# Opening a transformer step by quarters of the model width, and four changes of order behind it

## The chip, the cores and the metric

The kernel runs on one core of one Trainium2 chip. Its time is the device time in microseconds of one execution, and the figure for a kernel is the median of its runs. Engines go by the profile's names: PE is TensorE (PEld its weight loads), DVE is VectorE, ACT is ScalarE, POOL is GpSimd, and SP is the engine that issues the DMAs.

## What is computed

One step of a two-layer backbone for 384 tokens (128 context tokens, 256 latent tokens) of width 1024. Each layer is a SwiGLU FFN of inner width 2816, a mixer (gated linear recurrence, convolution, grouped attention, sharing one input and one output projection), and a second FFN. Every sub-layer is modulated by shift, scale and gate, which come from the conditioning vectors `c` (latents) and `c_ctx` (context):

```python
mod = (silu(cond) @ p["w_mod"] + p["b_mod"])
sh1, sc1, g1, sh2, sc2, g2, sh3, sc3, g3 = split(mod, 9)
f1 = swiglu(x * (1 + sc1) + sh1, ffn1_w_in, ffn1_w_out)
x  = layer_norm(ALPHA * x + 0.5 * g1 * f1)
y  = mixer(x * (1 + sc2) + sh2)
x  = layer_norm(ALPHA * x + g2 * y)
f2 = swiglu(x * (1 + sc3) + sh3, ffn2_w_in, ffn2_w_out)
x  = layer_norm(ALPHA * x + 0.5 * g3 * f2)
```

## The kernel before, in words

All operands are float32. A product is made of three float32r products: each operand is split into a rounded part and a rest, and high x high, high x low and low x high are added up. ScalarE casts a weight tile to its high part and VectorE subtracts to get the low part (`split_to`, L587 to L591); activations live as `xh` and `xl`, in columns of tokens, eight k-tiles of 128.

**Opening** (`setup` from L76, `first` from L261). The nine pieces of `mod` are each 1024 columns of w_mod. The first two of layer 0 (shift and scale of the first FFN) are wanted at once, so they come re-laid in four quarters `q` of two k-tiles, each in two halves of 1 MB (`w_mod_first`, loaded at L273). `gemv` (L276, products L283) multiplies them with the silu'd conditioning columns `cc` on TensorE, `row` (L294) adds the bias rows `brow`, a transpose (L300) makes columns, and `modulated` (L297 to L324) makes two k-tiles of `xh` and `xl` from `xT`, the transposed input. `xT` comes from 24 transposes of X on TensorE (L347). `products` (L326, through `aform`, matmuls at L599) adds a quarter to the gate and up products of hidden units 0 and 1; a unit is 128 hidden columns, an FFN has 22. The weights of units 0 and 1 are one pair's loads of 1 MB each for gate and up (L342).

**FFN** (`ffn`, from L684). Weights are loaded in pairs of units: gate and up (`load_gu`, L697) and rows of w_out (`load_o`, L702), 1 MB each, into four buffers `raw`. `prep(u)` (L706) splits what unit `u` needs, and for an even unit issues its pair's loads first. The loop at L794 does for each unit: `fill_ends` (finishes of w_mod pieces), `prep(u + 1)`, `fill(u)`, 24 matmuls each for gate and up (L803, L809), `act` (silu, product, split of the hidden tile; L762 to L769), and `out(u - 1)`, 18 matmuls of 512 columns into three accumulator pairs in PSUM (L612). The `out` of the last four units (`hold`) is put off to the end, where it covers the layer norm.

**Fillers**. The other w_mod pieces are made between the FFN's work by VectorE. A piece is eight `step`s (L180): for each k-tile a row tile `t` of w_mod (512 KB, L177) is multiplied by `cc` and added to `G`, for both conditionings, the first k with L198, the others with L200; each step asks for a later row. How many steps a unit gets is written out: `SLOW` is 2, 2, 2, 2 and `FAST` 3, 2, 3 (L42, `fill` at L1657). When the eighth step is done, `finish_job` (L205) adds up the partitions with 16 small matmuls on TensorE (L212), at the start of the next unit.

**Mixer** (`mixer`, from L838). The input projection runs in gemms of 128 columns; weights n = 0 to 15 are cast by `hi(n)` (L870) and subtracted by `lo(n)` (L876), into four buffers `wgu`. Gemms 4 to 7 are L599 products; the values and keys are 72 products of 512 columns (`wide_mm`, L672) with W8 to W11, W10 being first wanted after twelve of them. `Dec.sums` (L1063 to L1076) makes the decays of the recurrence, a scan on VectorE and three exponentials on ScalarE per direction; `dec[0]` and `dec[1]` are two halves of the heads. The order of all this is the order of the lines 1306 to 1373.

**What sets the order.** TensorE, VectorE, ScalarE and GpSimd execute in the order in which the program is written. Only the SP queue's order is chosen by a planner, which may put a DMA that waits for nothing ahead of one that waits for a buffer.

## Time and profile before

| | us |
|---|---|
| median of 3 runs | 1551.99 |
| lowest and highest | 1550.87, 1553.07 |
| profiled execution, its own time | 1551.26 |
| its span, first to last instruction | 1549.5 |
| TensorE busy with matmuls in the span | 1509.1 |
| VectorE busy | 1080.3 |
| ScalarE busy | 614.8 |

The profiled execution is one more run, taken by the hardware profiler. Its span begins with the first instruction and ends with the last; its own time is 1.76 us longer. Matmuls are pipelined, so a busy TensorE need not be at its full rate; the distance between the starts of two matmuls tells more than the busy share. "Idle before" in a row is the time in which the engine had nothing to do ahead of it, and the arrow names what ended it. The granted clock (PEclk) is a share of 2.4 GHz and has two levels, 1.0 and 0.5.

### The profile page before, as it was taken

The page shows a single profiled execution, that of the slowest core. Times are in us where ns is not written, and L with a number is a line of the kernel's source. Part 1 is how long each engine was busy: PE and PEld are TensorE (multiplying, and loading weights), DVE is VectorE, ACT ScalarE, POOL GpSimd, SP SyncE. Part 2 cuts the span into 40 slices and gives each one's busy share as a digit, 9 for nine tenths or more (in the row PEclk, how much of TensorE's full clock was granted, in tenths as well). Part 3 has the DMA queues.
Part 4 walks back from the last instruction along what each step waited for, and adds up shares of the span by engine and source line. Part 5 has one row for each costly group of instructions (what it writes and reads, how often), then busy time and mean ns, then how long its engine had stood idle before and what let it go on. Part 6 is the DMA issues. An engine that isn't in the chain of part 4 may idle for free. (4 is left out here: it accounts for less than half of the span.)

```text
span 1549.5 us, 23561 instructions
## 1 busy us (share of the span) xinstructions
PE 1509.1 (97%) x9575; PEld 1342.6 (87%) x9575; DVE 1080.3 (70%) x1546; ACT 614.8 (40%) x1069; POOL 59.1 (4%) x95
## 2 busy tenths in 40 slices
PE   7999999998999999999999999999989999999997
PEld 5989999888677899999989999998976689999996
DVE  4798878678667778877677676675776786554334
ACT  2333223266475522222253233233653763333331
POOL 0000000030101000000000000000201100000001
PEclk8999999999999999999999999999999999999999
DMA  8776757423434457665535464643326046442411
GB/s 359 288 267 227 245 193 253 167 77 122 98 108 163 164 204 245 219 229 195 215 109 217 163 245 167 240 156 117 118 73 188 28 165 244 149 176 110 163 55 41
DMA packets 63076, 269.65 MB, mean 174 GB/s; under 512 B 9128, under 2 KB 13688, under 8 KB 47864
## 3 DMA queue, kind: packets, MB, share of 16 engines
q1 hardware_dynamic: 62968, 268.15, 49.4%
q8 instruction: 75, 1.23, 0.3%
q14 instruction: 33, 0.27, 0.1%
HBM read 265.09 MB, written 3.03 MB: 173 GB/s over the span
## 5 line engine op out<-in xcount | busy, mean ns | idle before, releaser
L599 PE MATMUL w<-xh,wgu 128*128 128x384 f32 x2752 | 719.5, 337 | 0.9 <-DVE hf L766 0.9
L599 PEld LDWEIGHTS w<-xh,wgu 128*128 128x128 f32 x2752 | 499.5, 188 | 9.6 <-issue 4.5
L599 PE MATMUL w<-xl,wgu 128*128 128x384 f32 x1376 | 461.2, 335 | 0.0
L612 PE MATMUL d<-wo,hh 128*128 128x512 f32 x1056 | 284.5, 391 | 0.1
L200 DVE SCALAR_TENSOR_TENSOR G<-t,cc,G 128x1024 f32<-128x1024 f32 x224 | 272.9, 1279 | 0.0
L599 PEld LDWEIGHTS w<-xl,wgu 128*128 128x128 f32 x1376 | 259.3, 188 | 2.2
L590 DVE TENSOR_TENSOR wgu<-raw,wgu 128x1024 fp32r<-128x1024 f32 (+2 forms) x176 | 203.1, 1197 | 37.1 <-ACT wgu L589 37.0
L612 PEld LDWEIGHTS d<-wo,hh 128*128 128x128 f32 x1056 | 196.9, 188 | 36.9 <-ACT hh L768 0.4
L768 ACT CAST hh<-hf 128x384 fp32r<-128x384 f32 x82 | 42.2, 514 | 359.4 <-DVE hf L766 359.4
L589 ACT CAST wgu<-raw 128x1024 fp32r<-128x1024 f32 (+2 forms) x176 | 172.3, 1028 | 1.9 <-DMA raw<-ffn_w_in 1.8
L612 PE MATMUL d<-wo,hl 128*128 128x512 f32 x528 | 163.3, 391 | 0.0
L766 DVE TENSOR_TENSOR hf<-w,sg 128x384 f32<-128x384 f32 x80 | 44.4, 556 | 169.7 <-PE w L599 165.3
L764 ACT ACTIVATE sg<-w 128x384 f32<-128x384 f32 x80 | 39.2, 490 | 293.5 <-PE w L599 293.5
L590 DVE TENSOR_TENSOR wo<-raw,wo 128x1024 fp32r<-128x1024 f32 x90 | 109.6, 1219 | 14.4 <-ACT wo L589 14.4
L612 PEld LDWEIGHTS d<-wo,hl 128*128 128x128 f32 x528 | 99.1, 188 | 21.2
L672 PE MATMUL d<-wgu,xh 128*128 128x512 f32 x336 | 107.8, 402 | 8.7 <-ACT wgu L870 7.2
L589 ACT CAST wo<-raw 128x1024 fp32r<-128x1024 f32 x90 | 94.4, 1050 | 18.0 <-DMA raw<-ffn_w_out 16.5
L672 PEld LDWEIGHTS d<-wgu,xh 128*128 128x128 f32 x336 | 63.8, 192 | 23.6 <-ACT wgu L870 8.1
L769 DVE TENSOR_TENSOR hl<-hf,hh 128x384 fp32r<-128x384 f32 x82 | 45.8, 559 | 47.6 <-ACT hh L768 47.6
L672 PE MATMUL d<-wgu,xl 128*128 128x512 f32 x168 | 66.9, 398 | 0.0
L425 ACT ACTIVATE t<-w,colB,colA 128x128 f32<-128x128 f32 x120 | 43.5, 468 | 46.3 <-PE w L416 41.2
L599 PE MATMUL d<-xh,wgu 128*128 128x384 f32 x192 | 52.8, 350 | 2.2 <-ACT wgu L589 1.7
(272 smaller groups left out, 1412.1 us busy)
## 6 DMA issues: line engine op xcount, KB each, us to landing
raw<-ffn_w_in SPq DMA_DIRECT2D x82, 1024.0 KB
t<-w_mod SPq DMA_DIRECT2D x128, 512.0 KB
raw<-ffn_w_out SPq DMA_DIRECT2D x44, 1024.0 KB
raw<-w_in SPq DMA_DIRECT2D x12, 1024.0 KB
raw<-entry SPq DMA_DIRECT2D x10, 1024.0 KB
raw<-w_mod_first SPq DMA_DIRECT2D x8, 1024.0 KB
G<-gates SPq DMA_DIRECT2D x12, 512.0 KB
raw<-w_in_vk SPq DMA_DIRECT2D x4, 1024.0 KB
```

Of the source, the lines that this page charges most:

```text
L200: nc.vector.scalar_tensor_tensor(ac, raw, cc, ac, ALU.mult, ALU.add)
L425: self.nc.scalar.activation(m[:, k, :], pts[k // 4][:, k % 4 * P : (k % 4 + 1) * P], AF.Identity, scale=A[:, k, c : c + 1], bias=B[:, k, c ...
L589: nc.scalar.copy(w[:, 0], src)
L590: lo_engine.tensor_tensor(w[:, 1], src, w[:, 0].bitcast(F32), ALU.subtract)
L599: nc.tensor.matmul(ps, w[:, wi, k, :], x[:, k, :], start=(k == 0 and i == 0), stop=(k == KT - 1 and i == 2),)
L612: nc.tensor.matmul(acc[:, n, :], h, w[:, wi, n * 512 : n * 512 + 512], start=(first and i == 0), stop=(last and i == 2),)
L672: self.nc.tensor.matmul(ps, x[:, k, tok * P : (tok + 1) * P], w[k // 2][:, wi, k % 2, :], start=(k == 0 and i == 0), stop=(k == KT - 1 and ...
L764: nc.scalar.activation(sg, pg, AF.Silu)
L766: nc.vector.tensor_mul(hf, pu, sg)
L768: nc.scalar.copy(hh, hf)
L769: nc.vector.tensor_sub(hl, hf, hh.bitcast(F32))
```

## The change

The opening now makes units 0, 1 and 2. Their weights (384 columns of gate and up) and the transposed x come from two re-laid inputs in quarters, so the transposes of X are gone, and X itself is loaded at the start of the FFN. Each quarter loads two halves of w_mod, x and w_in. `products(q, part)` is one k-tile of all three units, 18 matmuls; the next quarter's splits, gemvs and row sum stand between its two parts. `warm(n)` puts n matmuls of a zero tile where TensorE would otherwise have none, 27 in all. `prep` of an odd unit now issues the next pair's loads at its end. In `step`, the first k of a piece is made by ScalarE. `LAST` takes the place of the last `SLOW` in two plans, and layer 0's first plan begins at unit 2 with 2, 3, 3. In the mixer, W10 and W11 are split ahead of `dec[1].sums`.

```diff
-SLOW, FAST = [2, 2, 2, 2], [3, 2, 3]
+SLOW, FAST, LAST = [2, 2, 2, 2], [3, 2, 3], [3, 3, 1, 1]
...
-        for tok in range(NT):
-            nc.sync.dma_start(
-                self.X[:, tok, :],
...
+        ahead()
         pt = self.wbank()
...
             if k == 0:
-                nc.vector.tensor_scalar_mul(ac, raw, cc)
+                nc.scalar.activation(ac, raw, AF.Copy, scale=cc)
...
+            def load_x(q):
+                nc.sync.dma_start(xT[:, 2 * q : 2 * q + 2, :], a["x_T"][q])
+            def load_wi(q):
+                nc.sync.dma_start(
+                    wi[:, q].rearrange("p i k n -> p (i k n)"), a["ffn1_w_in_first"][q]
+                )
...
+            raws = {(0, 0): load(0, 0)}
+            zero = self.t(self.gp, [P, P], "stage", bufs=3)
+            nc.gpsimd.memset(zero, 0.0)
+            units = [self.pair(i) for i in range(3)]
+            def warm(n):
+                for _ in range(n):
+                    nc.tensor.matmul(units[2][:, 1, 0:P], zero, zero, start=True, stop=True)
+            self.setup(lambda: warm(9))
+            warm(6)
+            raws[0, 1] = load(0, 1)
+            load_x(0)
+            load_wi(0)
...
                     nc.vector.tensor_sub(
                         self.xl[:, k, :], m[:, i, :], self.xh[:, k, :].bitcast(F32)
                     )
+                    if mid and i == 0:
+                        mid()
+            def products(q, part):
+                for u in range(3):
+                    for i in range(2):
+                        self.aform(units[u][:, i, 0:T], w[i][u], 2 * q + part, 8)
+                        yield
...
+            def splits(q):
+                ks = slice(2 * q, 2 * q + 2)
+                for u in range(3):
+                    for i in range(2):
+                        self.split_to(
+                            w[i][u][:, :, ks], wi[:, q, i, :, u * P : (u + 1) * P], nc.vector
+                        )
+            gemv(0, 0)
+            warm(4)
+            gemv(0, 1)
             row(0)
...
+            warm(2)
+            modulated(0, lambda: splits(0))
+            warm(6)
+            for q in range(4):
+                if q < 3:
+                    raws[q + 1, 0] = load(q + 1, 0)
+                    load_x(q + 1)
+                    load_wi(q + 1)
+                    raws[q + 1, 1] = load(q + 1, 1)
+                for _ in products(q, 0):
+                    pass
+                if q < 3:
+                    splits(q + 1)
+                    gemv(q + 1, 0)
+                    gemv(q + 1, 1)
+                    row(q + 1)
+                rest = products(q, 1)
+                next(rest)
+                next(rest)
+                if q < 3:
+                    modulated(q + 1)
+                for _ in rest:
+                    pass
...
             def prep(u, entry=False):
                 m, h = u // 2, u % 2
-                if h == 0:
-                    if not entry and ("g", m) not in raws:
-                        load_gu(m)
-                    if ("o", m) not in raws:
-                        load_o(m)
+                if ("o", m) not in raws:
+                    load_o(m)
...
+                if h == 1 and u + 1 < NU and ("g", m + 1) not in raws:
+                    load_gu(m + 1)
+                    load_o(m + 1)
...
             if first:
-                self.ord = [2, 0, 1]
-                acc = [self.pair(2)]
+                for tok in range(NT):
+                    nc.sync.dma_start(
+                        self.X[:, tok, :],
...
+                self.ord = [0, 1, 2]
                 load_o(0)
                 load_gu(1)
-                for u in range(2):
-                    prep(u, True)
-                for u in range(2):
+                acc = []
+                for u in range(3):
+                    if u < 2:
+                        prep(u, True)
                     act(u, eps[u][:, 0, 0:T], eps[u][:, 1, 0:T])
-                prep(2)
-                acc += [self.pair(0), self.pair(1)]
-                out(0, range(NT))
-                out(1, range(NT))
+                    acc.append(self.pair(u))
+                prep(2, True)
+                prep(3)
+                out(0, [0, 1])
+                out(1, [0, 1])
+                out(0, [2])
+                out(1, [2])
...
-            self.fill(1, fp)
-            for u in range(2, NU):
+            self.fill(2, fp) if first else None
+            for u in range(3 if first else 2, NU):
...
-        E += [dec[1].sums(0), dec[1].sums(1)]
...
         his[10] = hi(10)
+        lo(10)
         his[11] = hi(11)
-        lo(10)
+        lo(11)
+        E += [dec[1].sums(0), dec[1].sums(1)]
         dec[0].queries(0)
-        lo(11)
         dec[0].queries(1)
...
-            (0, 0): ([(0, p) for p in range(2, 8)], plan(1, SLOW, FAST, FAST, FAST, FAST, SLOW)),
-            (0, 2): ([(0, 8)] + [(1, p) for p in range(4)], plan(4, FAST, FAST, FAST, SLOW, SLOW)),
+            (0, 0): ([(0, p) for p in range(2, 8)], plan(2, [2, 3, 3], *[FAST] * 4, LAST)),
+            (0, 2): ([(0, 8)] + [(1, p) for p in range(4)], plan(4, FAST, FAST, FAST, SLOW, LAST)),
```

## Rows read from the trace of the kernel before

**Rows 1.** The page: the span, and busy time, share and instructions of each engine.

```profile
span 1549.5 us, 23561 instructions
...
PE 1509.1 (97%) x9575; PEld 1342.6 (87%) x9575; DVE 1080.3 (70%) x1546; ACT 614.8 (40%) x1069; POOL 59.1 (4%) x95
```

**Rows 2.** TensorE's waits: for whom, us in total, times, longest us.

```profile
PE d L672 <- ACT wgu L870: 7.2, 2, 3.6
...
PE w L212 <- DVE G L200: 4.1, 6, 1.1
```

**Rows 3.** Timeline of the opening: start us, us, what, [idle before <-releaser].

```profile
3.47 1.28 ACT L94 ACT_TABLE_LOAD   x1 [3.47 <-PE w L91]
...
13.97 1.93 PE L283 MATMUL w<-raw,cc 128*32 128x128 f32 x32 [1.67 <-DMA raw<-w_mod_first]
...
16.03 0.29 DVE L294 TENSOR_TENSOR rows<-w,brow 128x128 f32<-128x128 f32 x1 [4.05 <-PE w L283]
...
18.55 0.69 PE L599 MATMUL d<-xh,wgu 128*128 128x384 f32 x1 [1.70 <-ACT wgu L589]
...
19.59 4.90 DVE L590 TENSOR_TENSOR wgu<-raw,wgu 128x256 fp32r<-128x256 f32 x8
...
23.56 2.07 PE L283 MATMUL w<-raw,cc 128*32 128x128 f32 x64
```

**Rows 4.** Windows of the opening: busy by engine, then PEclk, DMA share, GB/s.

```profile
0.00:10.00 10.00, 4.72 (x22) 4.64 (x23) 0.82 (x2) 2.64 (x4) 1.31 (x13) 1.00 0.72 274
...
14.00:16.00 2.00, 1.90 (x32) 1.35 (x32) 0.00 (x0) 0.00 (x0) 0.00 (x0) 0.50 0.99 414
...
24.00:26.00 2.00, 2.00 (x62) 1.80 (x55) 0.78 (x2) 0.00 (x0) 0.00 (x0) 1.00 0.88 344
```

**Rows 5.** Timeline of TensorE, 55 to 73 us.

```profile
55.60 0.34 PE L599 MATMUL w<-xh,wgu 128*128 128x384 f32 x1
...
72.27 1.09 PE L612 MATMUL d<-wo,hh 128*128 128x512 f32 x4
```

**Rows 6.** Timelines of TensorE and VectorE at two finishes of a w_mod piece.

```profile
245.95 0.64 PE L212 MATMUL w<-G,sel 128*32 128x256 f32 x8 [0.44 <-DVE G L200]
...
285.85 4.87 DVE L200 SCALAR_TENSOR_TENSOR G<-t,cc,G 128x1024 f32<-128x1024 f32 x4
...
288.22 0.34 PE L599 MATMUL w<-xh,wgu 128*128 128x384 f32 x1
...
290.77 0.64 PE L212 MATMUL w<-G,sel 128*32 128x256 f32 x8 [0.46 <-DVE G L200]
...
291.34 0.44 PE L599 MATMUL w<-xh,wgu 128*128 128x384 f32 x1
```

**Rows 7.** Timelines of ScalarE, VectorE and TensorE in layer 0's mixer.

```profile
376.04 1.98 ACT L870 CAST wgu<-raw 128x1024 fp32r<-128x1024 f32 x2
...
370.27 1.22 DVE L876 TENSOR_TENSOR wgu<-raw,wgu 128x1024 fp32r<-128x1024 f32 x1
...
370.59 0.63 PE L672 MATMUL d<-wgu,xh 128*128 128x512 f32 x2
...
373.12 0.39 PE L672 MATMUL d<-wgu,xl 128*128 128x512 f32 x1
...
393.50 0.60 PE L1118 MATMUL w<-ident,da 128*128 128x128 f32 x4
```

**Rows 8.** Windows with the clock, columns as in rows 4.

```profile
380.00:382.00 2.00, 2.00 (x6) 1.38 (x5) 1.97 (x5) 0.41 (x3) 0.00 (x0) 0.50 0.00 0
...
764.00:766.00 2.00, 2.00 (x12) 2.00 (x9) 1.53 (x3) 2.00 (x3) 0.00 (x0) 0.64 1.02 408
...
766.00:768.00 2.00, 2.00 (x8) 2.00 (x7) 1.73 (x2) 0.28 (x1) 0.00 (x0) 0.51 0.95 293
```

**Rows 9.** Groups by line: busy us, mean ns, then idle before.

```profile
L198 DVE TENSOR_SCALAR G<-t,cc 128x1024 f32<-128x1024 f32 x32 | 22.6, 748 | 0.0
...
L589 ACT CAST wgu<-raw 128x1024 fp32r<-128x1024 f32 x168 | 167.9, 1048 | 1.8 <-DMA raw<-ffn_w_in 1.8
```

More of the change, by code (lines that the diff above doesn't have):

```diff
@@ L324, in modulated @@
                     )
-            def products(q, i, us=(0, 1)):
-                for u in us:
-                    self.aform(units[u][:, i, 0:T], w[i][u], q, 4)
-            src = a["b_mod"][0].rearrange("(x q e n) -> x e q n", q=4, e=2, n=P)
-            r0 = []
-            for h in range(2):
-                r0.append(load(0, h))
-                for j in (2 * h, 2 * h + 1):
-                    nc.sync.dma_start(
-                        self.brow[32 * j : 32 * j + 2, :].rearrange("p (q n) -> p q n", q=4),
-                        src[j // 2, j % 2].unsqueeze(0).to_broadcast([2, 4, P]),
-                    )
@@ L339, in first @@
-            raws = []
-            for i in range(2):
-                raw = self.t(self.rawp, [P, KT, 256], "raw")
-                nc.sync.dma_start(raw.rearrange("p k n -> p (k n)"), a["ffn1_w_in"][0, i, 0])
-                raws.append(raw)
-            for tok in range(NT):
-                pv = self.pair(tok).rearrange("p a (b t) -> p (a b) t", t=P)
-                for k in range(KT):
-                    nc.tensor.transpose(
-                        pv[:, k, :], self.X[:, tok, k * P : (k + 1) * P], self.ident
-                    )
-                for i, copy in enumerate((nc.scalar.copy, nc.vector.tensor_copy)):
-                    ks = slice(4 * i, 4 * i + 4)
-                    copy(xT[:, ks, tok * P : (tok + 1) * P], pv[:, ks, :])
@@ L353, in first @@
-            units = [self.pair(0), self.pair(1)]
-            for h in range(2):
-                gemv(0, h, r0[h])
-            row(0)
-            modulated(0)
-            w = [
-                [self.t(self.wgu, [P, 2, KT, P], "wgu", F32R) for u in range(2)] for i in range(2)
-            ]
-            for ks in (slice(0, 2), slice(2, KT)):
-                for i in range(2):
-                    for u in range(2):
-                        self.split_to(
-                            w[i][u][:, :, ks], raws[i][:, ks, u * P : (u + 1) * P], nc.vector
-                        )
@@ L804, in ffn @@
                 if u == 2:
-                    if not first:
-                        turn01(1)
-                        turn01(2)
-                        acc = [self.pair(i) for i in self.ord]
+                    turn01(1)
+                    turn01(2)
+                    acc = [self.pair(i) for i in self.ord]
                 self.aform(pu[:, 0:T], wu)
@@ L816, in ffn @@
                     next(rest, None)
-                if u == 2 and not first:
+                if u == 2:
                     out(0, range(NT))
-                if u - 1 < NU - hold and not (first and u == 2):
+                if u - 1 < NU - hold:
                     out(u - 1, range(NT))
```

54 lines of the change are left out of this document (21 added, 33 removed).

## The prediction

> **What bounds the kernel now.** The page's engine table comes first: matrix multiplies occupy TensorE 97% of the span, VectorE 70% [rows 1]. So time can only be won where TensorE waits, or runs at the lower clock, or is given less to do; none of the edits takes matmuls away except the 24 transposes of X. The list of TensorE's waits is the second view: outside the opening it has two large entries, the mixer's first wide products behind ScalarE (7.2 us in two waits, one per layer) and the finish of a w_mod piece behind VectorE (4.1 us in six) [rows 2]. The third view is the timeline of the opening, where single rows show what each step waits for [rows 3], with its windows for the clock and the DMA rate [rows 4]. Weights show up nowhere in the FFN loops as something TensorE waited for.
>
> **The change, part by part.** The sum is made against the profiled execution, 1551.26 us, which is 0.73 us under the median of 1551.99.
>
> *Opening.* The mark on both sides is the start of unit 3's gate product, since units 0 to 2 and the `out` of units 0 and 1 lie ahead of it in both kernels. Before: 96 products of units 2 and 3 fill 55.60 to 72.27 [rows 5], 0.1736 us each, so unit 3 begins at 72.27 - 48 x 0.1736 = 63.9.
>
> After, the first work needs w_mod's first half (1.05 MB, now issued first), then ident and c. The engines move 414 GB/s once they run in the opening [rows 4], so 1.05 MB takes 2.5 us; with some 2.7 us until the first bytes flow (an estimate from the first transpose, which started 0.3 us ahead of the table load at 3.47 [rows 3]) c is there at about 5.4. Transpose, table load of 1.28 us and Silu put the first gemv at 7.3. It doesn't decide: the first row sum needs `brow`, whose four small loads now stand behind both w_mod halves, x and the first quarter of w_in, 3.28 MB or 7.9 us: about 11.3. From the row sum to the first product was 2.5 us (16.03 to 18.55 [rows 3]): first product at 13.8, where it was 18.55. The 27 warming matmuls lie in waits for c, for the table, for brow and for VectorE; I cost them at nothing, and at most at 27 x 0.17 = 4.7 us, if each lasted like a product and all stood on the path.
>
> Then VectorE paces: it subtracted 8 pieces of 128x256 in 4.90 us [rows 3], 0.61 each, so a quarter's 6 take 3.7. Products of k=0 end at about 17.9; xh and xl of k=1 take about 1 (part of the 3.6 below); the next quarter's splits stand ahead of the row sum in VectorE's order, so row(1) ends at 22.8, and TensorE, through with its gemvs and two products at 21.4, waits 1.4. From there a quarter costs TensorE 36 x 0.1736 = 6.25, two gemvs 2.07 [rows 3] and 0.2 for the transpose, 8.5 us; VectorE 3.7 + 3.6 (16.03 to 19.59 [rows 3]) = 7.3; DMA 3.28 MB = 7.9. TensorE is last of the three, so row(3) comes at 22.8 + 17.0 = 39.8, and the remaining 48 products end at 48.3. At the turn to `out`, act, the split of wo and the freeing of the second pair cost a wait of about 1.3 us (an estimate, bounds 0 and 4), then 36 products of 0.23 us [rows 7], 8.3: unit 3 at 57.9. **Saved: 6.0 us.** X, loaded later, is first read in the tail; o0 and the next gate and up rows land by about 46, ahead of their use.
>
> The first w_mod piece now runs in three units (2, 3, 3 steps) where it had four of 2. A step is two VectorE operations of 1.22 (4.87 for four [rows 6]). Three steps are 7.3 us, three subtractions of the splits at the same 1.22 are 3.7, act some 2: VectorE needs about 13 where TensorE's 48 products and 18 of `out` take 12.5, so I let the piece's finish wait 0.8 us longer than now: net for the opening **5.3 us** (bounds 1.5 and 8).
>
> *Weights ahead of w_mod rows.* The SP queue issues g, u and o of the next pair before the rows. They wait for raw buffers that the splits of the same `prep` free, and those splits stand ahead of the fill's steps on VectorE too, so the rows behind are late by issue time alone. No TensorE wait names them: 0, bounds -1 and +2.
>
> *k=0 on ScalarE.* Per piece VectorE loses 2 x 0.748 us, ScalarE gains two operations like its 128x1024 cast, 1.05 each [rows 9]; it is idle most of the time. VectorE's k=1 step can begin when the first half is there. The one wait in the middle of the FFN that this frees is the piece end near 246, 0.44 us [rows 6]: **0.4 us**, bounds 0 and 2.
>
> The Trainium skill ("ScalarE: Activation LUTs", Rules for kernel authors) says to put multiplications on VectorE rather than ScalarE. By that rule this part would cost time (rival 3); the rows agree that the operation itself is slower there, 1.05 against 0.75.
>
> *Last piece thinned.* In the last units TensorE has no `out`, so a unit is 48 products, 8.3 us, while VectorE has two steps and the splits. At 288.4 TensorE reaches the piece's finish; VectorE works on its four operations until 290.7; the last product starts at 288.22 and the next at 291.34 [rows 6]. Undisturbed the finish takes twice the 0.57 us of its second half, so 1.8 us are lost. With one step in units 19 and 20 VectorE ends there 2.4 us earlier, by about 288.3; unit 18's third step pushes the next splits back by the same 2.4 us, and a whole unit of 8.3 us lies between these and their use. The same finish in layer 0's second FFN waits alike (both are among the six of [rows 2]), and there the clock stood at 0.64 and 0.51 in the two windows after it [rows 8], about 3.4 us at half rate, 1.7 lost: 1.8 + 1.8 + 1.7 = **5.3 us**, bounds 2.5 and 5.8.
>
> *Values' weights ahead of the second decays.* 72 products run from 370.59 to 393.50, 22.9 us; the first eleven keep 0.23 (370.59 to 373.12), so undisturbed they take 16.5. The wait is for ScalarE's casts of W10 and W11 at 376.04, which stand behind the second exponentials; then VectorE's subtraction; then a stretch at clock 0.50 [rows 7, 8]. After: W10's cast follows that of W9 at 369.3, W11's can start when gemm 7 ends, 370.8; VectorE, through with W9 at 371.4 [rows 7], has W10 at 372.5 and W11 at 373.7, and TensorE wants them at 373.3 and 374.7. No wait: 6.4 us, twice **12.8**. Late next are the decays, 2.3 us later than now on VectorE; they are first used in its keys behind the splits of W12 and W13, and those wait for buffers that the same wide products free, earlier by as much. Bounds 4 each (a wait of 2 stays) and 6.6.
>
> Sum: 5.3 + 0 + 0.4 + 5.3 + 12.8 = 23.8; 1551.3 - 23.8 = 1527.5, with 0.7 to the median: **1528.2 us**.
>
> **The rivals.**
> 1. *The opening at half clock.* Before, TensorE fell to 0.50 when it had waited for w_mod, and 32 gemv matmuls then took 1.93 us, and the first products were half as fast, until near 24 us [rows 3, 4]. If the warming doesn't hold it, 18 products take 6.2 us instead of the 4.1 that VectorE paces, two gemvs 3.9 instead of 2.1, less the wait of 1.4 that this fills: 2.5 us more, 1530.7. For it: TensorE still waits often until 14 us; against: warming matmuls fill the gaps. By the page "TensorE: Matmul & The Clock Gate" of the Trainium skill (What's actually happening) the low clock is the default and activity lifts it. The trace disagrees for the start, 1.00 in the first 10 us [rows 4], and agrees later.
> 2. *SP's order.* X (1.57 MB, 3.7 us) has no buffer to wait for; if it is issued ahead of the last w_mod quarters, these land after TensorE wants them, and the first rows may stand behind the second pair: 2 to 6 us, 1532.
> 3. *ScalarE's k=0 on the path.* It stands ahead of silu, and VectorE's k=1 waits for it; 2.1 against 1.5 us in each of 16 pieces would be 9.6 less won: 1537.8. The skill's rule on multiplications, named above, speaks for it. Against: VectorE's subtraction of wo ends about when the first half does.
> 4. *The mixer's wait comes back* at the states or scores, whose inputs VectorE now makes later, and all 12.8 us are lost again: 1541.0. For: VectorE has work without a gap from W9 on, 70% over the span [rows 1]; against: what is put later is only 2.3 us late, and its users move by 6.4.
> 5. *Slower: rows starved behind weights.* At the SP queue three 1 MB loads, 7.5 us, stand ahead of the rows; were the rows late in all 11 densely filled pieces, each finish would make TensorE wait. From 23.8 / 11 = 2.2 us a piece on nothing is won; at 4 us a piece, 1572.2. Against: four rows are loaded ahead, over a unit's work.
>
> **How the numbers follow.** Forecast 0.73; rivals 0.11, 0.07, 0.04, 0.035, 0.015. The range takes in the forecast's own bounds (opening 1.5 to 8, clock and order) and the first three rivals nearly: 1521 to 1537. About 0.2%, 3 us, is what a measurement can tell from no change; only rival 5 and a collapse of several parts come near it: faster 0.97, same 0.015, slower 0.015.
>
> **What would show it.** Right: first product near 14 and unit 3's start near 58; no wait of TensorE for W10's cast, the 72 wide products in 16.5 us; the finishes ahead of unit 21 in about 1.2 us, with the clock at 1.00 through both. Wrong: granted clock of 0.5 between 13 and 24 us, finishes that wait for VectorE by over 2 us, or weights named among TensorE's waits.

## The result, and the profile after

| | before | after |
|---|---|---|
| median of 6 runs each, us | 1553.26 | 1535.08 |
| lowest and highest | 1550.87, 1558.80 | 1532.87, 1538.02 |
| profiled execution, its own time | 1551.26 | 1536.88 |
| its span | 1549.5 | 1535.1 |

The ratio is 0.9878, with a 95% interval of 0.9856 to 0.9899: 18.2 us between the medians, 14.4 between the two profiled executions. Five more runs of the changed kernel beside the experiments gave a median of 1534.82; over all eleven the median is 1534.82 too, and that is what the experiments below are compared with. The experiments ran on three chips, on which the kernel before has medians of 1552.26, 1553.18 and 1553.79, so a difference of medians below can carry 1.5 us from that alone.

The page of the changed kernel, rows as in [rows 1]:

```profile
span 1535.1 us, 23662 instructions
...
PE 1508.9 (98%) x9605; PEld 1343.1 (87%) x9605; DVE 1058.8 (69%) x1525; ACT 649.2 (42%) x1112; POOL 59.2 (4%) x96
```

TensorE is busy as long as before, in a span 14.4 us shorter; what went is, on balance, waiting. Its list of waits, as in [rows 2], shows which:

```profile
PE w L208 <- DVE G L196: 2.5, 1, 2.5
...
PE d L623 <- DVE hf L777: 1.5, 1, 1.5
...
PE w L610 <- DVE hf L777: 1.4, 2, 0.9
```

The 7.2 us behind ScalarE's casts are gone, and of the six waits at finishes one is left. But that one is 2.5 us, where the longest of the six was 1.1, and two waits for `hf`, 1.47 at the turn to `out` and 0.87 in unit 4, stand where before had none. Where they lie, TensorE's timeline tells:

```profile
14.94 0.45 PE L610 MATMUL d<-xh,wgu 128*128 128x384 f32 x1 [0.30 <-ACT wgu L600]
...
51.29 1.19 PE L623 MATMUL d<-wo,hh 128*128 128x512 f32 x4 [1.47 <-DVE hf L777]
...
58.23 0.34 PE L610 MATMUL w<-xh,wgu 128*128 128x384 f32 x1
...
75.91 0.45 PE L610 MATMUL w<-xh,wgu 128*128 128x384 f32 x1 [0.87 <-DVE hf L777]
...
87.00 2.28 PE L208 MATMUL w<-G,sel 128*32 128x256 f32 x16 [2.54 <-DVE G L196]
...
124.94 0.63 PE L623 MATMUL d<-wo,hh 128*128 128x512 f32 x2
...
288.14 1.07 PE L208 MATMUL w<-G,sel 128*32 128x256 f32 x16
...
368.34 0.63 PE L683 MATMUL d<-wgu,xh 128*128 128x512 f32 x2
...
384.71 0.60 PE L1136 MATMUL w<-ident,da 128*128 128x128 f32 x4
```

Unit 3 starts at 58.23, 5.7 us earlier than the 63.9 of before: the opening did what it should. The `out` of unit 6 starts at 124.94, where it stood at 124.64 before: 67 us later nothing is left of the 5.7. (A second profile of the changed kernel, from the last experiment below, has 123.46; there 1.2 us are left.) The finish ahead of unit 21 runs through in 1.07 without a wait (288.14; before it was cut in two, [rows 6]), and the wide products of layer 0's mixer take 16.4 us, 368.34 to 384.71, where they took 22.9 [rows 7].

What VectorE and ScalarE did between unit 3's start and the finish at 87:

```profile
58.92 2.47 DVE L196 SCALAR_TENSOR_TENSOR G<-t,cc,G 128x1024 f32<-128x1024 f32 x2
...
65.90 1.05 ACT L600 CAST wo<-raw 128x1024 fp32r<-128x1024 f32 x1 [2.98 <-DMA raw<-ffn_w_out]
...
66.98 1.22 DVE L601 TENSOR_TENSOR wo<-raw,wo 128x1024 fp32r<-128x1024 f32 x1 [2.80 <-ACT wo L600]
...
68.12 7.26 DVE L196 SCALAR_TENSOR_TENSOR G<-t,cc,G 128x1024 f32<-128x1024 f32 x6
...
80.79 7.26 DVE L196 SCALAR_TENSOR_TENSOR G<-t,cc,G 128x1024 f32<-128x1024 f32 x6
```

VectorE stands idle for 2.80 us, because unit 4's `wo` has not landed, and then has two units of three steps; the last six operations end at 88. (The two operations of a piece's first k are now ScalarE's, L194, and not in this list.) And the clock, in the windows of the opening, of that finish and of the scores of the mixer (columns as in [rows 4]):

```profile
10.00:16.00 6.00, 4.67 (x56) 3.63 (x55) 2.85 (x10) 2.40 (x7) 0.00 (x0) 1.00 1.02 419
16.00:24.00 8.00, 7.18 (x94) 6.42 (x93) 5.41 (x17) 3.06 (x10) 0.00 (x0) 1.00 1.02 418
...
88.00:90.00 2.00, 1.88 (x14) 1.02 (x11) 1.42 (x4) 1.45 (x2) 0.00 (x0) 0.50 1.01 414
90.00:92.00 2.00, 2.00 (x8) 2.00 (x8) 1.41 (x2) 1.06 (x2) 0.00 (x0) 0.50 1.02 416
...
402.00:404.00 2.00, 2.00 (x16) 0.59 (x12) 1.97 (x8) 0.51 (x2) 0.00 (x0) 0.50 1.07 215
1162.00:1164.00 2.00, 2.00 (x16) 0.68 (x17) 0.00 (x0) 0.00 (x0) 0.00 (x0) 0.50 0.62 127
```

The fall of before between 14 and 24 us is gone. Behind the wait at 84 to 87, in which TensorE did nothing, there is a new one, and in both layers' mixers the granted clock falls later, in the scores, where it was 1.00 before; by windows of 2 us that costs 1.7 us in each layer, as much as the fall in the wide products cost before [rows 8].

### The profile page after: what moved, and what is told of

Its sections match the earlier page's. It is cut to its first block, busy times and chain, and to the rows that moved or that the text cites. A ratio compares the mean times of both kernels' runs of the same rounds, so it can differ in the third digit from the quotient of the medians.

```text
span 1535.1 us, 23662 instructions
## 1 busy us (share of the span) xinstructions
PE 1508.9 (98%) x9605; PEld 1343.1 (87%) x9605; DVE 1058.8 (69%) x1525; ACT 649.2 (42%) x1112; POOL 59.2 (4%) x96
## 4 chain that ended last, share of the span: by engine, by line
PE 92%; ACT 2%; DVE 2%; DMA 2%; issue 1%; SPq 0%; POOL 0%; DVEq 0%; POOLq 0%; ACTq 0%
PE w L610 45%; PE d L623 26%; PE d L683 7%; PE d L610 4%; PE w L1004 2%; PE w L664 1%; PE w L208 1%; PE d L1195 1%; PE w L427 1%; PE d L1229 1%; ACT Pr L1463 1%; DVE G L196 1%; PE d L1445 1%; PE d L1493 1%; DMA wi<-ffn_w_in_first 1%
## 5 line engine op out<-in xcount | busy, mean ns | idle before, releaser
L610 PE MATMUL w<-xh,wgu 128*128 128x384 f32 x2720 | 711.6, 337 | 1.4 <-DVE hf L777 1.4
L610 PEld LDWEIGHTS w<-xh,wgu 128*128 128x128 f32 x2720 | 494.0, 188 | 10.9 <-issue 4.9
L610 PE MATMUL w<-xl,wgu 128*128 128x384 f32 x1360 | 455.7, 335 | 0.0
L601 DVE TENSOR_TENSOR wgu<-raw,wgu 128x1024 fp32r<-128x1024 f32 x166 | 196.1, 1222 | 39.1 <-ACT wgu L600 38.6
L600 ACT CAST wgu<-raw 128x1024 fp32r<-128x1024 f32 x166 | 166.2, 1049 | 3.4 <-DMA raw<-ffn_w_in 3.4
L683 PE MATMUL d<-wgu,xh 128*128 128x512 f32 x336 | 104.6, 392 | 0.0
L600 ACT CAST wo<-raw 128x1024 fp32r<-128x1024 f32 x90 | 94.4, 1049 | 11.7 <-DMA raw<-ffn_w_out 11.3
L683 PEld LDWEIGHTS d<-wgu,xh 128*128 128x128 f32 x336 | 62.3, 188 | 12.5
L486 POOL TENSOR_TENSOR st<-st,eps 128x1 f32<-128x1 f32 x18 | 8.0, 445 | 1202.0 <-ACT X L482 1202.0
```

What stands on the lines that cost most here:

```text
L600: nc.scalar.copy(w[:, 0], src)
L601: lo_engine.tensor_tensor(w[:, 1], src, w[:, 0].bitcast(F32), ALU.subtract)
L610: nc.tensor.matmul(ps, w[:, wi, k, :], x[:, k, :], start=(k == 0 and i == 0), stop=(k == KT - 1 and i == 2),)
L683: self.nc.tensor.matmul(ps, x[:, k, tok * P : (tok + 1) * P], w[k // 2][:, wi, k % 2, :], start=(k == 0 and i == 0), stop=(k == KT - 1 and ...
```

## The experiments

Each kernel is the changed one, or the one before, with one thing different, or with several where that is said. Ratios are to runs of the kernel before on the same chip; the changed kernel itself stands at 0.9878 in the result and at 0.9883 in its five later runs. "Unit 6" is the start of that unit's `out`, the common mark in the traces: 124.64 before, 124.94 and 123.46 in the two profiles of the changed kernel.

**The mixer's order alone.** The kernel before with

```diff
-        E += [dec[1].sums(0), dec[1].sums(1)]
...
         his[10] = hi(10)
+        lo(10)
         his[11] = hi(11)
-        lo(10)
+        lo(11)
+        E += [dec[1].sums(0), dec[1].sums(1)]
         dec[0].queries(0)
-        lo(11)
```

> The kernel before with one edit alone: the splits of W10 and W11 stand ahead of the second decays. Theory (the prediction's mixer term, corrected by the trace of the changed kernel): the waits for W10 go, so the 72 wide products take about 16.5 us where they took 22.9, 6.4 us less in each layer; then the granted clock falls once more inside the scores, which takes back 0 to 3 us per layer. So 8 to 13 us faster in all, 0.9916 to 0.995 of the time before. Rival: the wait only moves to the states or scores, whose inputs VectorE now makes later; then the wide products are 6.4 us shorter, PE waits for VectorE there by as much, and the time is within 2 us of before.

Measured: 1540.40 (1539.75 to 1541.97), ratio 0.9918 [0.9901, 0.9935], 11.9 us less than before. By TensorE's timeline the wide products run from 372.43 to 388.80, 16.4 us again:

```profile
372.43 0.63 PE L672 MATMUL d<-wgu,xh 128*128 128x512 f32 x2
...
388.80 0.60 PE L1118 MATMUL w<-ident,da 128*128 128x128 f32 x4
```

The window of the scores behind them, columns as in [rows 4]:

```profile
396.00:412.00 16.00, 14.79 (x394) 9.52 (x393) 12.54 (x41) 6.77 (x20) 4.45 (x6) 1.00 0.82 187
```

The clock stays at 1.00 there and in the second layer's scores, so this order doesn't bring the fall every time; of the ten traces with this order and the new opening nine show it, in one layer or both, and why is open. This term of the prediction holds nearly whole: 11.9 of 12.8.

**The opening alone.** The changed kernel with the other four parts put back (VectorE's k=0, the old order of the loads, `SLOW` for `LAST`, the old order in the mixer; each edit stands below by itself or above).

> The changed kernel with only its opening kept (three units by quarters, first w_mod piece in steps of 2, 3, 3); order of the loads, VectorE's k=0, the last piece's steps and the mixer's order are those of before. Theory: unit 3 starts 5.7 us earlier than before, but the first w_mod piece then makes PE wait for VectorE some 4 us ahead of unit 5, and a fall of the granted clock behind that wait takes 0 to 2 us more: at the end 0 to 2 us faster than before, ratio 0.9985 to 1.0. Rival (the prediction's own term): 5.3 us of the opening last to the end, ratio 0.9966, and what was lost in the changed kernel was lost through the order of the loads or k=0 on ScalarE.

Measured: 1558.33 (1556.91 to 1562.51), ratio 1.0040 [1.0026, 1.0053]. Neither theory: it is 6 us slower than before, and 5.7 late at unit 6 (130.38). Unit 3 starts at 58.29, as in the changed kernel; then, in the timelines of ScalarE and TensorE:

```profile
69.48 1.05 ACT L600 CAST wgu<-raw 128x1024 fp32r<-128x1024 f32 x1 [10.52 <-DMA raw<-ffn_w_in]
...
73.66 0.44 PE L610 MATMUL w<-xh,wgu 128*128 128x384 f32 x1 [2.75 <-ACT sg L775]
...
82.17 0.69 PE L610 MATMUL w<-xh,wgu 128*128 128x384 f32 x1 [2.47 <-DVE hf L777]
```

ScalarE waits 10.52 us for the next pair's up rows, and TensorE waits behind it twice. So a part that I had put at nothing, the order of the loads, became the suspect, and the next run undoes it by itself.

**The old order of the loads.** The changed kernel with

```diff
-                if ("o", m) not in raws:
-                    load_o(m)
+                if h == 0:
+                    if not entry and ("g", m) not in raws:
+                        load_gu(m)
+                    if ("o", m) not in raws:
+                        load_o(m)
...
-                if h == 1 and u + 1 < NU and ("g", m + 1) not in raws:
-                    load_gu(m + 1)
-                    load_o(m + 1)
```

> The changed kernel with the loads in the order of before: the next pair's g, u and o are issued at the start of the next pair's first unit, behind the w_mod rows. Theory (formed on the run with the opening alone): a row's issue waits until VectorE has freed a row buffer, and everything behind it in SP's queue waits with it; right after the opening VectorE is late, so the third pair's weights are issued late and PE waits for their casts, 2.9 us near 70 and 2.6 us near 79, with the clock falling behind each. 5 to 9 us slower than the changed kernel, some 1540 to 1544 us. Rival (the prediction's own 0 for this part): within 2 us of the changed kernel, and the loss in the run with the opening alone came from k=0 on VectorE or from the last piece's steps.

Measured: 1540.54 (1536.78 to 1545.70), ratio 0.9918 [0.9895, 0.9941]; 5.7 us more than the changed kernel. The timelines of SP's queue (its issues), ScalarE and TensorE:

```profile
52.62 0.35 SPq L708 DMA_DIRECT2D raw<-ffn_w_in  x1
60.51 2.44 SPq L173 DMA_DIRECT2D t<-w_mod  x2
63.00 0.42 SPq L708 DMA_DIRECT2D raw<-ffn_w_in  x1
...
69.28 1.05 ACT L600 CAST wgu<-raw 128x1024 fp32r<-128x1024 f32 x1 [7.86 <-DMA raw<-ffn_w_in]
...
81.85 0.44 PE L610 MATMUL w<-xh,wgu 128*128 128x384 f32 x1 [4.08 <-DVE hf L777]
```

And a window of the same kernel:

```profile
58.00:62.00 4.00, 4.00 (x22) 3.72 (x22) 4.00 (x4) 3.42 (x4) 0.00 (x0) 1.00 0.18 25
```

From 58 to 62 the DMA engines move 25 GB/s: nothing is issued, since the next things in the queue are two w_mod rows, and the up rows and `wo` of units 4 and 5 stand behind them. The rows wait for buffers that the first two steps of the piece free, ScalarE's at 60.5 and VectorE's at 62.6. In the changed kernel these weights are issued at 56.76 and 57.90, and the same window moves 324 GB/s. At unit 6 this kernel (128.53) is 3.6 and 5.1 us behind the two profiles of the changed one. So the first theory holds: with the new opening this order is worth some 4 to 6 us. The kernel before has the same queue, and its timelines of SP and VectorE show the same lateness one engine further back:

```profile
63.27 0.71 SPq L697 DMA_DIRECT2D raw<-ffn_w_in  x1
65.24 0.33 SPq L177 DMA_DIRECT2D t<-w_mod  x1
65.66 0.39 SPq L702 DMA_DIRECT2D raw<-ffn_w_out  x1
...
73.86 1.23 DVE L590 TENSOR_TENSOR wo<-raw,wo 128x1024 fp32r<-128x1024 f32 x1 [2.57 <-ACT wo L589]
```

VectorE stood idle for 2.57 us there too; with two steps a unit it still came in time, and TensorE had nothing to show for it in this execution. In the run with the mixer's order alone, whose program is the same up to the mixer, it had: 1.66 us for `hf` at 81.39.

**The first piece over four units.** The changed kernel with

```diff
-            (0, 0): ([(0, p) for p in range(2, 8)], plan(2, [2, 3, 3], *[FAST] * 4, LAST)),
+            (0, 0): ([(0, p) for p in range(2, 8)], plan(2, SLOW, *[FAST] * 4, [3, 3, 2])),
```

> The changed kernel with the first w_mod piece over four units of two steps (as before the change) instead of 2, 3, 3, and the last piece in 3, 3, 2 to make room. Theory: the waits for VectorE at the end of the first piece (2.70 and 0.74 us) and the fall of the clock behind them (6.8 us at half rate, 3.4 us lost) come from the six steps that VectorE has in two units; with two steps a unit they go: 3.5 to 7 us less by 95 us into the span. The last finish has two steps ahead of it again and waits 1.8 us as before. Net against the changed kernel 1.7 to 5 us faster. Rival: VectorE is late because the third pair's wo lands late and its split stands ahead of all steps; then the wait stays whatever the steps are, nothing is won at 95 us, and the time is 0 to 2 us more than that of the changed kernel.

Measured: 1536.68 (1534.66 to 1541.93), ratio 0.9898 [0.9878, 0.9919]; no faster than the changed kernel. TensorE's timeline shows both halves of the theory, the second larger than expected:

```profile
119.12 1.09 PE L623 MATMUL d<-wo,hh 128*128 128x512 f32 x4
...
285.83 2.19 PE L208 MATMUL w<-G,sel 128*32 128x256 f32 x16 [3.44 <-DVE G L196]
```

Unit 6 stands at 119.12, 5.5 us earlier than before: with two steps a unit the opening's gain is kept to the end of the first piece and beyond, to the `out` of unit 17 (261.25, 267.62 before). Then the last piece, in three units instead of four, makes TensorE wait 3.44 us, and the clock falls behind that (0.55 from 288 to 292). That names a cause. The 48 steps were spread over 20 units; the new opening takes one of these units, with its room for two steps, out of the loop. In both spreads, the piece that had to do with three units instead of four made TensorE wait.

**Three, three, two.** The third step of the first piece goes where VectorE stood idle for 2.80 us, ahead of unit 4's `wo` (the expectation calls it unit 3's); the changed kernel with

```diff
-            (0, 0): ([(0, p) for p in range(2, 8)], plan(2, [2, 3, 3], *[FAST] * 4, LAST)),
+            (0, 0): ([(0, p) for p in range(2, 8)], plan(2, [3, 3, 2], *[FAST] * 4, LAST)),
```

> The changed kernel with the first w_mod piece in steps of 3, 3, 2 instead of 2, 3, 3. Theory: VectorE stands idle for 2.7 us ahead of unit 3's wo, which waits for its load; the third step moved there costs nothing, and the last unit of the piece has two steps, so the finish waits 0.3 to 0.6 us where it waited 2.7: 2.4 us less, and 3.3 us more where the fall of the clock behind that wait goes too. 2 to 6 us faster than the changed kernel, some 1529 to 1533 us. Rival: the third row isn't there in time (its load is issued near 51 us behind 5 MB of weights), VectorE waits for it ahead of the weights' splits, and unit 4 starts later: 0 to 4 us slower.

Measured: 1533.95 (1531.47 to 1538.95), ratio 0.9876 [0.9852, 0.9899]: within the scatter of the changed kernel. TensorE's timeline is better there:

```profile
84.24 0.64 PE L208 MATMUL w<-G,sel 128*32 128x256 f32 x8 [0.15 <-DVE G L196]
85.44 0.64 PE L208 MATMUL w<-G,sel 128*32 128x256 f32 x8 [0.56 <-DVE G L196]
...
120.01 0.39 PE L623 MATMUL d<-wo,hh 128*128 128x512 f32 x1
```

And the window behind the finish:

```profile
88.00:90.00 2.00, 2.00 (x14) 2.00 (x13) 1.23 (x1) 0.31 (x1) 0.00 (x0) 1.00 0.96 397
```

The finish hardly waits, the clock behind it stays at 1.00, and unit 6 comes 4.9 and 3.5 us earlier than in the two profiles of the changed kernel. The second piece's finish then waits in two parts, which brings the changed kernel back by 1.3. At the first `out` of the held units, behind all pieces of this FFN, 3, 3, 2 stands at 294.05, the changed kernel at 297.71 and 296.24, the kernel without the opening (next) at 295.90 and the kernel before at 299.91. So the same three units lose much less with the steps in this order. The execution as a whole took 1534.40 us, between the two of the changed kernel, 1536.88 and 1533.61: what is won at 88 shows in the traces, and is smaller than the scatter of the median.

**The opening taken out.** The kernel before with every part of the change but the opening: the mixer's order and the order of the loads as in the diffs above, and

```diff
-                nc.vector.tensor_scalar_mul(ac, raw, cc)
+                nc.scalar.activation(ac, raw, AF.Copy, scale=cc)
...
-            (0, 0): ([(0, p) for p in range(2, 8)], plan(1, SLOW, FAST, FAST, FAST, FAST, SLOW)),
-            (0, 2): ([(0, 8)] + [(1, p) for p in range(4)], plan(4, FAST, FAST, FAST, SLOW, SLOW)),
+            (0, 0): ([(0, p) for p in range(2, 8)], plan(1, SLOW, FAST, FAST, FAST, FAST, LAST)),
+            (0, 2): ([(0, 8)] + [(1, p) for p in range(4)], plan(4, FAST, FAST, FAST, SLOW, LAST)),
```

> The kernel before with every part of the change except the opening: mixer order, k=0 on ScalarE, weights loaded ahead of the rows, last piece in steps of 3, 3, 1, 1. Theory: the opening wins 5.7 us by unit 3, and the first w_mod piece gives nearly all of it back, so without the opening the time is that of the changed kernel within 2.5 us: 1533 to 1537.5. It is the mixer-order run (1540.4) less 3.7 for the two last finishes, less 0 to 1.7 for the clock there, less 0.4. Rival (the prediction's own term): the opening is worth 5.3 us in the end, so 1540 us or more.

Measured: 1531.82 (1530.38 to 1536.83), ratio 0.9864 [0.9843, 0.9885]. Were the opening worth its 5.3 us, this would be 0.9912, outside the interval. Its median is 3 us under the changed kernel's, but the intervals overlap: an estimate from both of them puts the opening, as it stands in the changed kernel, between 2.5 us gained and 6.8 lost. So it is shown not to bring its 5.3, and not shown to cost anything. TensorE has no wait at all in the trace of this kernel between 56 and 130, and unit 6 stands at 123.12, where the changed kernel has 124.94 and 123.46. The median is 3 to 4 us lower than the sum of the other parts in the expectation, and no run says why; VectorE's wait for `wo` is 1.26 there instead of 2.57, so the new order of the loads may be worth something behind the old opening too, but no run has it alone.

**The last piece in 2, 2, 2, 2.** The changed kernel with

```diff
-            (0, 0): ([(0, p) for p in range(2, 8)], plan(2, [2, 3, 3], *[FAST] * 4, LAST)),
-            (0, 2): ([(0, 8)] + [(1, p) for p in range(4)], plan(4, FAST, FAST, FAST, SLOW, LAST)),
+            (0, 0): ([(0, p) for p in range(2, 8)], plan(2, [2, 3, 3], *[FAST] * 4, SLOW)),
+            (0, 2): ([(0, 8)] + [(1, p) for p in range(4)], plan(4, FAST, FAST, FAST, SLOW, SLOW)),
```

> The changed kernel with the last w_mod piece of both filled FFNs in steps of 2, 2, 2, 2 again. Theory: both finishes ahead of unit 21 wait some 1.8 us for VectorE again, and the clock falls behind one or both of them (1.5 us each): 3.7 to 6.7 us slower than the changed kernel, 1538.5 to 1541.5. Rival: the finish's place makes the clock fall elsewhere anyway, and only 3 us or less are lost.

Measured: 1538.75 (1537.50 to 1541.12), ratio 0.9905 [0.9886, 0.9923]; 3.9 us more than the changed kernel by the medians, though the intervals overlap. In TensorE's timeline the finish waits as before, and alike in the second FFN:

```profile
288.02 0.64 PE L208 MATMUL w<-G,sel 128*32 128x256 f32 x8 [1.10 <-DVE G L196]
289.12 0.64 PE L208 MATMUL w<-G,sel 128*32 128x256 f32 x8 [0.47 <-DVE G L196]
...
756.24 0.64 PE L208 MATMUL w<-G,sel 128*32 128x256 f32 x8 [1.10 <-DVE G L196]
```

From the last product ahead of the finish to the first one behind it 3.1 us pass (286.58 to 289.69), where it is 1.3 in the changed kernel (287.87 to 289.14). Twice 1.8 is 3.6: the prediction's two waits are right. No fall of the clock followed either of them in this trace. Over all traces it did behind 3 of the 8 finishes that have these waits (at 764 before, at 292 in the mixer's order alone, at 296 in the opening alone), at 1.7 us each, and behind none of the 19 last finishes that `LAST` thins. So the prediction's clock term is borne out in kind, and is on the average of these traces about 1.3 us.

**VectorE's k=0.** The changed kernel with

```diff
-                nc.scalar.activation(ac, raw, AF.Copy, scale=cc)
+                nc.vector.tensor_scalar_mul(ac, raw, cc)
```

> The changed kernel with the k=0 products of each w_mod piece back on VectorE (two operations of 0.75 us per piece). Theory: in the evenly filled pieces nothing waits on it but the finish near 245 (0.3 to 0.4 us); in the first piece VectorE stands idle for its third pair's wo anyway (2.4 us), so the 1.5 us mostly vanish there: 0.4 to 1.5 us slower than the changed kernel. Rival: VectorE is short in the opening's first piece, so 1.5 us more there bring a longer wait and a longer stretch at low clock, 3 us or more. Other rival (ScalarE on the path): faster than the changed kernel.

Measured: 1536.81 (1535.75 to 1537.26), ratio 0.9890 [0.9870, 0.9910]; 2.0 more than the changed kernel, not told apart from it. In the trace, whose clock is at half for 6.8 us behind the first piece as in the changed kernel's first profile, unit 6 stands 0.1 later than there; VectorE's idle time ahead of `wo` is 1.68 there instead of 2.80, as the first theory has it. The wait at 245.95 that the edit was to free is gone here too, and in the run with the mixer's order alone, both with VectorE's k=0; so nothing shows that the edit freed it. That ScalarE's k=0 would be on the path, 9.6 us, is not borne out.

**Without the warming matmuls**, twice. The changed kernel with

```diff
-                for _ in range(n):
-                    nc.tensor.matmul(units[2][:, 1, 0:P], zero, zero, start=True, stop=True)
+                return
```

> The changed kernel without its 27 warming matmuls. Theory: the granted clock then falls to 0.50 somewhere between 8 and 25 us, as it did before the change after PE had waited for w_mod, and the gemvs and first products take twice as long for that stretch: first product near 15, but the second row later, 1.5 to 5 us slower at the end of the opening. Rival: the clock holds without them, since the gemvs and products now come earlier and closer together; then the opening is the same within 0.5 us.

> The same kernel as the run without the warming matmuls, profiled once more. There two of six runs took 1534.5 to 1535.5 us, as the changed kernel, and four took 1540.6 to 1542.8, and the profile was of a short one: its granted clock was at half for a stretch near 15.6 to 17.8 us and the opening ended at the same time. Theory: in the long executions the clock stays at half for much longer in the opening, 4 to 8 us later at unit 3; a profile of one shows it. Rival: the opening is alike in all, and the long ones lose it in falls of the clock behind the first w_mod piece and in the scores.

Measured: 1540.81 (1534.53 to 1542.84) and 1538.10 (1532.84 to 1540.27), ratios 0.9908 [0.9885, 0.9932] and 0.9895 [0.9874, 0.9916]. The windows of the opening in the second of the profiles:

```profile
12.00:16.00 4.00, 1.40 (x4) 1.07 (x5) 2.86 (x10) 2.41 (x7) 0.00 (x0) 0.78 1.01 418
16.00:20.00 4.00, 4.00 (x14) 4.00 (x14) 3.97 (x12) 2.34 (x8) 0.00 (x0) 0.50 1.02 428
```

So the warming does hold the clock: without it TensorE, which had been busy for 1.40 of the 4 us from 12 to 16, ran the first products at 0.50, in both profiles; in none of the traces with warming does the clock fall there. It cost 1.4 us at the first `out` in this execution (49.63 against 48.26) and nothing in the other, where the stretch at half was shorter and the wait that follows took it up.

The warming did one thing more, which the clock's column doesn't show. TensorE's timelines of the first gemvs, without warming (the first profile) and in the changed kernel:

```profile
8.32 3.42 PE L302 MATMUL w<-raw,cc 128*32 128x128 f32 x64 [1.62 <-ACT cc L90]
```

```profile
8.12 1.08 PE L303 MATMUL w<-raw,cc 128*32 128x128 f32 x32
```

The merged rows hide the single matmuls, whose starts tell more. With warming 32 of them take 1.08 us, 0.11 for four; without it four take 0.21 until 11.3. Four take 0.21 where the kernel before has them at 0.50 (1.93 for 32 at 13.97 [rows 3]). So without warming TensorE began at the lower clock, though the column has 1.00 from 8 to 12, and the warming matmuls themselves stand 0.21 apart up to 4.6 and 0.11 from 6.65 on. By the same spacing the kernel before began low too: its transposes of X stand 0.21 apart from 5.54 to 10.08, in the window that shows 1.00 [rows 4]. It cost nothing in these traces, since the first row sum waits for `brow`.

The other 2 to 6 us of the medians are not in the opening of these two traces, and neither profile was of a run above 1538: the theory of 4 to 8 us in the opening is not shown, and where the long runs lose their time stays open.

**The subtractions of wo on GpSimd.** The 3, 3, 2 kernel with

```diff
-                lo = nc.vector
+                lo = nc.gpsimd if first and u in (3, 4, 5, 6) else nc.vector
```

> The run with the first piece in 3, 3, 2 and one edit more: the subtractions of wo for units 3 to 6 go from VectorE to GpSimd, four of 1.22 us, in the stretch where VectorE is short; the first of them is needed only 10 us later. Theory: VectorE's work in units 3 to 8 sets the time there, so the waits of the first and second pieces' finishes (0.3 and 0.9 us near 84, 0.65 twice near 125) and of hf near 74.7 (0.7) shrink or go: 1 to 2.5 us faster than 3, 3, 2 alone, some 1531 to 1533 us. Rival: GpSimd needs several us for each subtraction or slows VectorE while it runs, and out of unit 3 waits for it: same or slower, 1534 to 1540.

Measured: 1536.49 (1535.10 to 1540.63), ratio 0.9893 [0.9874, 0.9913]; unit 6 comes 4.2 us later than in the 3, 3, 2 kernel. The groups by line from 56 to 130 (busy us, mean ns, idle before):

```profile
L196 DVE SCALAR_TENSOR_TENSOR G<-t,cc,G 128x1024 f32<-128x1024 f32 x28 | 40.8, 1520 | 3.0 <-ACT G L194 2.3 <-DMA t<-w_mod 0.7
...
L601 POOL TENSOR_TENSOR wo<-raw,wo 128x1024 fp32r<-128x1024 f32 x4 | 10.8, 2695 | 87.7 <-ACT wo L600 87.7
```

The timelines of GpSimd and VectorE around one of the four:

```profile
80.09 2.67 POOL L601 TENSOR_TENSOR wo<-raw,wo 128x1024 fp32r<-128x1024 f32 x1 [11.00 <-ACT wo L600]
...
80.42 3.42 DVE L196 SCALAR_TENSOR_TENSOR G<-t,cc,G 128x1024 f32<-128x1024 f32 x1
```

GpSimd takes 2.70 us where VectorE takes 1.22, and the mean of the operations of VectorE's steps goes from 1278 ns to 1520: 28 of them cost 6.8 us more, and 4.9 were to be saved. The mean hides how. 24 of the 28 keep their 1.28; the four that begin while GpSimd subtracts take 2.48 to 3.42, and each of them ends 1.08 us after the subtraction (82.76 and 83.84 in the rows). So VectorE doesn't go slower beside GpSimd: its operation stands until the other is through. The rival holds.

**The changed kernel once more**, with nothing edited.

> The changed kernel once more, as the base that the other runs on this chip are compared with. Its six runs lay in two groups, 1536.2 to 1538.0 at a mean granted clock of 0.993 and 1532.9 to 1534.0 at 0.995 to 0.996. Theory: the difference of some 3.5 us is the fall of the clock behind the first w_mod piece's wait (6.8 us at half rate), which doesn't come in every execution; then runs lie in the same two groups again. Rival: the groups are those of the chips or the hour, and here all runs lie in one.

Measured: 1532.35 to 1539.17, median 1534.82, mean clocks from 0.992 to 0.995: the whole scatter on one chip. But the profile of a 1533.61 run has the fall behind the first piece too, only shorter: 2 us windows from 86 to 94 show 1.00, 0.57, 0.58, 1.00, where the first profile showed 0.65, 0.50, 0.50, 0.64. So the groups aren't "fall" and "no fall"; how long it lasts differs, and the falls in the scores differ as well. The first profile without warming, where the opening ended at the same time, has nearly the same waits at the first piece and no fall. The three stand at unit 6 as the lengths of the fall have it: 124.94 with 6.8 us at half, 123.46 with 3.4, 122.74 with none.

## Why the prediction was right, and where it was not

The forecast was 1528.2, the range 1521 to 1537, and the median 1535.1 lies in it. The sign and most of the size were right; 18.2 us were won where 23.8 were summed. One of the signs that it had named for being wrong did show, a finish that waits for VectorE by over 2 us. Step by step:

- **Opening, start of unit 3.** Right nearly to the row: first gemv 8.1 (7.3 forecast), first product 14.9 (13.8), last product 48.3 (48.3), wait at the turn 1.5 (1.3), unit 3 at 58.2 (57.9). The first product is late because `brow` is: the first row sum starts at 12.6, where 11.3 was reckoned.
- **Opening, net 5.3.** The step that failed. (6.0 less 0.8 is 5.2; the sum carries 5.3.) I let the first piece's finish wait 0.8 us longer than the 0.6 of before; it waits 2.5 us and `hf` ahead of it 0.9, and the clock falls behind the wait, which costs up to 3.4 us more (6.8 us at half) and which the term left out. Of the 5.7, between nothing and 1.9 us is left at unit 6, by the length of the fall. VectorE's work in a unit of three steps, 13 us against TensorE's 12.5, was worked out as if VectorE never had to wait: it stood idle 2.80 us for a weight that lands late, and two three-step units could not make up for that. The runs put about 0 in the place of 5.3 (no opening: 1531.8), and show why: the opening's unit had carried two of the 48 steps, and the steps stood in the wrong units. With 3, 3, 2 the finish waits 0.7 and the clock doesn't fall behind it.
- **Weights ahead of w_mod rows, 0.** Wrong behind the new opening, by 4 to 6 us. I read TensorE's waits of before, which name no weights, and not VectorE's, which has 2.57 us of idle time for `wo` at 73.86. A row that waits for its buffer holds everything behind it in SP's queue; before, with two steps a unit, VectorE mostly still came in time, and behind the new opening, with three in the units that follow, it does not. Without this edit the change would have been 5.7 us worse.
- **k=0 on ScalarE, 0.4.** Not contradicted, and not shown: 2.0 us between medians that scatter by more, 0.1 at unit 6 in the trace, and the wait that it was to free is gone without the edit too. The operation on ScalarE takes 1.15 us (group L194), not the 1.05 of the cast.
- **Last piece thinned, 5.3.** The two waits, 3.6, are right (by the trace; 3.9 by the medians). The 1.7 for the clock was one fall in every execution; without the edit it comes behind 3 of 8 finishes, with it behind none of 19, so about 1.3.
- **Mixer, 12.8.** 11.9 measured alone; the wide products are 6.5 us shorter in each layer. In the changed kernel's profile the clock takes 1.7 of that back in each layer's scores, which no term had; why it falls there is open.
- **The rivals.** The half clock in the opening is what the warming prevents. That the trace disagrees for the start of the kernel, as the first rival has it, is a misreading: the column shows 1.00, the spacing of the matmuls half the clock. And the queue's order is where rival 2 looked, though not X but w_mod rows held the weights. Rows starved behind weights did not show: in the changed kernel VectorE's steps are never kept waiting for a row. ScalarE's k=0 on the path (9.6 us) and the mixer's wait coming back are both ruled out by their runs.

Where the rest went can be followed along the two profiled executions, 14.4 us apart where 23.8 were summed. From the start to the first held `out` of layer 0's first FFN (299.91 before, 297.71 after) 2.2 us are won, where the opening, k=0 and one thinned piece were to bring 7.5. From there to the first `out` of its second FFN (531.77, 524.48) 5.1, where the mixer's order was to bring 6.4; in that FFN, to its first held `out` (774.14, 763.43), 3.4 of 3.5; in the rest 3.7 of 6.4. So 5.3 are missing in the FFN behind the opening and 4.0 around the two mixers, of which the clock in the scores is 3.4. That is one pair of executions, and the medians scatter by several us.

No version tried beats the changed kernel by more than the scatter; the one without the opening has the lowest median.

## What to carry to other kernels

A stage made shorter gives its time back where another engine had been using it: before counting a gain at the head of a loop, count the filler work that was spread over the units that went, and who is idle for what when it is squeezed into fewer. In these runs the place of a DMA in the issuing queue cost nothing only as long as nothing ahead of it waited for a buffer, so a change that shifts the freeing of one buffer changes the price of the order of all that follow. And where an expected gain is of the size of one fall of the clock, take it from the traces at a common mark, not from two medians.

## What the runs showed of the hardware

GpSimd and VectorE did not add up: beside each of four subtractions on GpSimd, of 2.41 to 2.86 us, one operation of VectorE's steps took 2.48 to 3.42 us instead of 1.28, and ended 1.08 us after the subtraction. The Trainium skill ("Trainium Architecture — The Big Picture", What this means for kernel authors) says that of the engines only these two contend, for a shared pair of ports, and that one locks the other out instead of sharing the bandwidth; the trace agrees, with the same 1.08 us in all four cases.

The same wait of TensorE brought a fall of the granted clock in one execution and not in another. Behind the 2.5 us at the first piece's finish the changed kernel fell to 0.50 for some 6.8 us in one profile (windows of 2 us with 0.65, 0.50, 0.50, 0.64: 1.4 + 2 + 2 + 1.4) and for 3.4 in the other (0.57, 0.58); the first profile without warming has the same wait (2.54, and 0.56 in the middle of the finish) and 1.00 throughout the windows from 84 to 94. Behind the waits of 1.1 and 0.5 us at the last finishes it fell in the kernel before at 764 [rows 8] and not at 290, and did not fall at 288 and 756 in the run with 2, 2, 2, 2.

The profile's clock column showed 1.00 at the start of the kernel while matmuls ran at half the pace: without warming four gemv matmuls took 0.21 us until 11.3 us, and in the kernel before four take 0.11 at 1.00 (from 11.21) and 0.21 at 0.50 (from 13.97).
